# Two-layer hybrid decoder trunk: the memory keys and values of each layer move from the start of the program into the z products of their layer

## The chip, the cores and the metric

The kernel runs on one core of one Trainium2 chip. The metric is the device time of one execution in microseconds, the median of several runs, lower is better. A core has TensorE (PE in the profile, with its weight loads as PEld), VectorE (DVE), ScalarE (ACT), GpSimd (POOL) and SyncE (SP), which here does nothing but issue DMAs. Each engine works through its own list of instructions in the order in which the program was built, and waits where an operand isn't there yet.

## The reference, cut to what matters

```python
def reference(x, mem, ...):
    for l in range(DEPTH):                                   # 2 layers
        h = rms_norm(x, norm_mix_w[l])                       # x: 1024 tokens x 1024
        x = x + hybrid_mixer(h, w_in[l], ...)                # ONE combined projection, three head groups
        hq = rms_norm(x, norm_xq_w[l])
        mem_n = rms_norm(mem, norm_mem_w[l])                 # mem: 256 tokens x 1024, the same in both layers
        x = x + memory_cross_attention(hq, mem_n, w_mq[l], w_mk[l], w_mv[l], w_mo[l])
    return rms_norm(x, final_norm_w)

def memory_cross_attention(h, mem_n, wq, wk, wv, wo):
    k = (mem_n @ wk).reshape(b, m, MEM_HEADS, MEM_HEAD_DIM)  # the memory keys
    v = (mem_n @ wv).reshape(b, m, MEM_HEADS, MEM_HEAD_DIM)  # the memory values
    ...
```

The memory keys and values depend on nothing but `mem` and weights, so they can be computed at any time before the cross-attention of their layer. The mixer's combined projection gives, among others, the values of two attention groups (V), the inputs of the forget gates and time steps, and z, the gate of the state-space group, which is not wanted until that group's output is gated.

## The kernel before, in words

**Products.** Every float32 operand is split into a high and a low half (`hi` on ACT, L77 or, with a scale, L79; `lo` = operand minus `hi`, L85 on POOL or DVE, L83 on DVE with a scale), and a product is three matmuls, high by high, low by high, high by low (`mm3`, L111 to L113; in `tokmaj` L372 to L374). Weights come through `wload`: one 128x1024 tile in two halves of 256 KB, DMA to `wst`, cast to `whi`, the rest to `wlo`. The normed activations of all 1024 tokens are kept as `hhi` and `hlo`, 8 slices k of 128 channels each.

**Order.** `body` runs `start`, then per layer `tokmaj`, `mixer`, `tail`. PE's order is fixed by the program: `weave(main, fill)` runs generators that yield after a few matmuls the time these take; `ratio` says how much of the fill is laid between steps of the main, and with `drain=False` what is left of the fill goes on later. The other engines' lists, SP's included, are laid out by the builder from a simulated timeline. SP issues the DMAs one after another, with up to 8 of them in flight; one that waits holds up all behind it.

**`start` (L1497).** First comes the memory: one tile of `w_mk`, `memT` in four pieces of 256 KB into `mt` (kept for both layers), `memkv(0)` and then `memkv(1)` as the fill under `norms()`. `norms` computes the memory's sums of squares (`memnorm`, L1192), loads x in two halves of eight 256 KB tiles, and norms each half (`norm_half`: squares on ACT, sums on DVE, matmuls with `onecol` L221, then `spread`: a power on POOL L234, diagonals on DVE, a matmul with `ones` L251; then `normed`, whose `lo` alternates between POOL and DVE). `memkv` (L1229) per layer: 8 key tiles of 24 matmuls 128x256, then 4 value pieces for 2 chunks of memory tokens, 24 matmuls each, 384 in all; into the `acc` and `big` buffers of PSUM; the weights alternate between the common pool (`wst`, `whi`, `wlo`) and one of its own (`xst`, `xhi`, `xlo`), and `alt_w` puts the `lo` of every second half on DVE. The results go to DRAM (`mk_hi`, `mk_lo`, `mv_hi`, `mv_lo`).

**`tokmaj` (L346).** Weights of five pieces (`load(pc)`: four DMAs `tms`, casts `tmh` on ACT, rests `tml` on POOL; pieces 0 and 1 are V, 2 to 4 are z). Each piece is multiplied for eight chunks of 128 tokens, 24 matmuls each, alternating between `acc` and `big`. V of tokens 0 to 511 (`values(0)`) is woven with a pending norm, then V of the rest, then `gates` with z as fill, which is drained at the end. A chunk of z is evacuated by a tanh on ACT (L392) and a DVE step (L393) into `zt`, and stored by SP (`z_st`). `gates` ends with sixteen stores of its rows `gar` to `sr_st` and `sl_st`.

Of the kernel before, what the change touches and what calls it, by code (L numbers as in the profile page):

```python
# [16 lines left out]
P = 128  # L17
D = 1024
T = 1024
L = 2  # L20
# [23 lines left out]
class Net:  # L44
# [49 lines left out]
    def wload(self, src, pool=None, first=None):  # L94
        parts = []
        for s in range(2):
            wp, tag, n = (self.wp, "w", 5) if pool is None else (pool, "x", 3)
            st = self.tile(wp, [P, 512], F32, tag + "st", 3)
            self.dma(st, src[:, s * 512 : (s + 1) * 512])
            if first is not None and s == 0:  # L100
                self.dma(first, self.a["memT"][:, 0:2, :])
            hi = self.tile(wp, [P, 512], F32R, tag + "hi", n)
            lo = self.tile(wp, [P, 512], F32R, tag + "lo", n)
            self.hi(hi, st)
            self.lo(lo, st, hi, eng=self.nc.vector if self.alt_w and s or first is not None else self.nc.gpsimd)
            parts.append((hi, lo))
        return parts
# [237 lines left out]
    def tokmaj(self, l, pools, first, norm):  # L345
# [3 lines left out]
        with self.pool("tm", 2, side="right") as pool:  # L349
# [56 lines left out]

            load(0)
            load(1)
            self.run(first)
            self.ratio, self.nb, self.alt_w = 0.0, 1, False  # L410
            self.weave(norm, values(0))
            pools.close()
# [3 lines left out]
            self.weave(self.gates(l), gate_z())  # L416
# [775 lines left out]
    def memnorm(self, pool, tmp):  # L1192
        nc = self.nc
        mt = self.mt
        nch = MT // P
        sums = []
        for k in range(0, KT, 2):
            sq = [self.tile(tmp, [P, MT], F32, "msq", 8) for _ in range(2)]
            nc.scalar.activation(sq[0], mt[:, k, :], AF.Square)
            nc.gpsimd.tensor_tensor(out=sq[1], in0=mt[:, k + 1, :], in1=mt[:, k + 1, :], op=ALU.mult)  # L1200
            nc.vector.tensor_tensor(out=sq[0], in0=sq[0], in1=sq[1], op=ALU.add)
            sums.append(sq[0])
# [6 lines left out]
        self.mrr = yield from self.spread(tmp, ps, nch, self.tile(pool, [P, MT], F32, "mrr", 1))  # L1209
# [3 lines left out]
    def memw(self, l, pool):  # L1213
        w = self.mw[l]
        if l == 0:

            nhi, nlo = (h[:, :, HALF : HALF + MT] for h in (self.hhi, self.hlo))
        else:
            nhi, nlo = (self.tile(pool, [P, KT, MT], F32R, n, 1) for n in ("nhi", "nlo"))
        for k in range(KT):  # L1220
            self.hi(nhi[:, k, :], self.mt[:, k, :], w[:, k : k + 1])
            self.lo(nlo[:, k, :], self.mt[:, k, :], nhi[:, k, :], w[:, k : k + 1])
        return nhi, nlo


    def memkv(self, l, pool, w0):
        nc, a = self.nc, self.a
        mm = nc.tensor.matmul
        nhi, nlo = self.memw(l, pool) if l == 0 else self.mnext  # L1229
        todo = []  # L1230

        def acc(i):
            return self.acc() if i % 2 else self.big()

        def keys(t, ps):
# [8 lines left out]

        def values(pc, c, ps):
            r = self.mrs[:, c : c + 1]
            vh = self.tile(pool, [P, MT], F32R, "kh")
            vl = self.tile(pool, [P, MT], F32R, "kl")
            self.hi(vh, ps, r)
            self.lo(vl, ps, vh, r)  # L1250
            self.dma(self.mvDs[l][0][:, c, pc * MT : (pc + 1) * MT], vh)
            self.dma(self.mvDs[l][1][:, c, pc * MT : (pc + 1) * MT], vl)

        def put(fn, *args):
            todo.append((fn, args))
            while todo and self.mrr is not None:
                g, b = todo.pop(0)
                g(*b)

        for t in range(KT):  # L1260
            ws = w0[t] if t < len(w0) else self.wload(a["w_mk"][l, t], (None, pool)[t % 2])
            ps = acc(t)[:, :MT]
            for k in range(KT):
                whi, wlo = ws[k // 4]
                s = slice((k % 4) * P, (k % 4 + 1) * P)
                self.mm3(ps, whi[:, s], wlo[:, s], nhi[:, k, :], nlo[:, k, :], k == 0, k == KT - 1)
                yield 0.33
            put(keys, t, ps)
        if l + 1 < L:
            self.dma(self.mw[l + 1], a["norm_mem_w"][l + 1])  # L1270
            self.mnext = self.memw(l + 1, pool)
        for pc in range(4):
            ws = self.wload(a["w_mv"][l, pc, 0]) + self.wload(a["w_mv"][l, pc, 1], pool)
            for c in range(2):
                ps = acc(c)[:, :MT]
                cs = slice(c * P, (c + 1) * P)
                for k in range(KT):
                    whi, wlo = ws[k // 2]
                    s = slice((k % 2) * MT, (k % 2 + 1) * MT)
                    mm(ps, nhi[:, k, cs], whi[:, s], start=k == 0, stop=False)  # L1280
                    mm(ps, nhi[:, k, cs], wlo[:, s], start=False, stop=False)
                    mm(ps, nlo[:, k, cs], whi[:, s], start=False, stop=k == KT - 1)
                    yield 0.33
                put(values, pc, c, ps)
# [338 lines left out]
```

## Time and profile before

| | |
|---|---|
| time, median of 3 runs | 2539.09 us (2537.62 to 2541.44) |
| the profiled execution's own time | 2551.32 us |
| its span in the profile | 2549.3 us |
| mean granted clock of TensorE | 0.984 |
| busy PE / DVE / ACT / POOL | 97% / 61% / 47% / 46% |
| first V product of layer 0 | 143.8 us |
| end of the gates, layer 0 and layer 1 | 228.9 and 1424.6 us |

Times are counted from the start of the span. A row of a timeline gives the start in us, the duration in us, the engine, the line of the program, the operation, result<-operands, the tile and how many of them came in a row; in square brackets stands how long the engine had idled before and what ended that. A row of grouped instructions gives their count, then the busy time in us and the mean of one in ns, then the idle time before them and what ended it. A row of windows gives the stretch, its length, the busy time of PE, PEld, DVE, ACT and POOL (with their instructions), the granted clock of TensorE (1.00 is full), the mean busy share of the 16 DMA engines and what they moved in GB/s.

### The profile page before, as it was taken

Reading aid. Unit: us, or ns where it says so; the run is one execution under the profiler, and the core shown is the slowest. Engines: PE = TensorE matmul, PEld = TensorE weight load, DVE = VectorE, ACT = ScalarE, POOL = GpSimd, SP = SyncE. Lnnn points to the kernel's source line nnn. Section 1 sums busy time; section 2 is a strip of 40 time slices with the busy share of each in tenths; the row PEclk is TensorE's granted clock in tenths of the full one; section 3 lists DMA queues with packets and bytes.
Section 4 is the critical chain, followed back from the end, with each engine's and each line's share of the span. In section 5 each row is a group of like instructions: output and inputs, shape, how many; then the busy total and the mean of one; then the engine's idle time right before and its main releaser. Section 6 shows DMA issues by size and latency. Waiting matters only on the chain.

```text
span 2549.3 us, 39348 instructions
## 1 busy us (share of the span) xinstructions
PE 2466.7 (97%) x13900; PEld 2081.7 (82%) x13900; DVE 1545.4 (61%) x2716; ACT 1189.0 (47%) x2455; POOL 1166.9 (46%) x1193
## 2 busy tenths in 40 slices
PE   8799999999999999999999999999999999999997
PEld 7799988888788777888879988888877877787886
DVE  6923166666778688654464226666668868764355
ACT  5532155545556455434443225455546645543442
POOL 5732144435566487432252124444446657732233
PEclk9999999999999999999999999999999999999999
DMA  7774132222222766553464223222223376554333
GB/s 235 217 237 111 65 98 70 66 88 86 81 87 90 246 221 195 162 169 116 128 195 120 78 68 92 70 79 84 89 71 90 115 256 209 170 185 151 119 93 132
DMA packets 230360, 333.37 MB, mean 131 GB/s; under 512 B 24370, under 2 KB 107442, under 8 KB 230148
## 3 DMA queue, kind: packets, MB, share of 16 engines
q1 hardware_dynamic: 228292, 328.76, 41.4%
q8 instruction: 110, 1.80, 0.3%
q10 hardware_dynamic: 1872, 2.10, 0.2%
q14 instruction: 86, 0.70, 0.1%
HBM read 238.72 MB, written 86.81 MB: 128 GB/s over the span
## 4 chain that ended last, share of the span: by engine, by line
PE 78%; DVE 7%; DMA 5%; issue 3%; ACT 3%; POOL 3%; SPq 1%; DVEq 0%; POOLq 0%; ACTq 0%
PE acc L111 16%; PE acc L112 15%; PE acc L113 15%; PE tp L667 3%; PE tp L630 2%; PE acc L372 2%; PE big L372 2%; PE acc L374 2%; PE big L374 2%; PE acc L373 2%; PE big L373 2%; SPq L72 1%; PE big L598 1%; PE big L599 1%; PE s L1128 1%
## 5 line engine op out<-in xcount | busy, mean ns | idle before, releaser
L111 PE MATMUL acc<-hhi,whi 128*128 128x512 f32 (+1 forms) x1960 | 796.8, 407 | 6.8 <-DVE th L510 5.4
L113 PE MATMUL acc<-hlo,whi 128*128 128x512 f32 (+1 forms) x1960 | 772.0, 394 | 0.0
L112 PE MATMUL acc<-hhi,wlo 128*128 128x512 f32 (+1 forms) x1960 | 771.6, 394 | 0.0
L85 POOL TENSOR_TENSOR wlo<-wst,whi 128x512 fp32r<-128x512 f32 x279 | 377.5, 1353 | 337.5 <-ACT whi L77 280.7
L113 PEld LDWEIGHTS acc<-hlo,whi 128*128 128x128 f32 x1960 | 372.0, 190 | 82.2
L111 PEld LDWEIGHTS acc<-hhi,whi 128*128 128x128 f32 x1960 | 374.2, 191 | 67.3 <-DVE th L510 5.8
L112 PEld LDWEIGHTS acc<-hhi,wlo 128*128 128x128 f32 x1960 | 373.8, 191 | 57.7
L77 ACT CAST whi<-wst 128x512 fp32r<-128x512 f32 x420 | 259.5, 618 | 302.8 <-PE acc L113 206.0
L77 ACT CAST ph<-tp 128x512 fp32r<-128x512 f32 (+1 forms) x256 | 142.5, 556 | 168.8 <-PE tp L630 118.0
L85 DVE TENSOR_TENSOR pl<-tp,ph 128x512 fp32r<-128x512 f32 (+1 forms) x256 | 167.0, 652 | 78.3 <-ACT ph L77 76.3
L85 DVE TENSOR_TENSOR wlo<-wst,whi 128x512 fp32r<-128x512 f32 x141 | 128.4, 910 | 118.0 <-ACT whi L77 117.2
L609 POOL TENSOR_SCALAR Pt<-Pt,sm 128x128 f32<-128x128 f32 (+7 forms) x128 | 105.8, 827 | 182.6 <-DVE sm L608 180.0
L1015 DVE SCALAR_TENSOR_TENSOR ac<-u,cw,ac 128x512 f32<-128x512 f32 x144 | 129.4, 899 | 34.0 <-POOL ac L1010 32.6
L85 POOL TENSOR_TENSOR tml<-tms,tmh 128x684 fp32r<-128x684 f32 (+3 forms) x40 | 67.4, 1703 | 132.7 <-ACT tmh L77 126.8
L607 ACT ACTIVATE Pt<-big,sm 128x128 f32<-128x128 f32 (+7 forms) x128 | 95.2, 743 | 69.8 <-DVE sm L605 62.3
L604 DVE TENSOR_REDUCE sm<-big 128x1 f32<-128x128 f32 (+7 forms) x128 | 96.1, 751 | 23.0 <-PE big L601 21.7
L372 PE MATMUL acc<-tmh,hhi 128*128 128x342 f32 (+3 forms) x320 | 102.1, 319 | 0.0
L372 PE MATMUL big<-tmh,hhi 128*128 128x342 f32 (+3 forms) x320 | 101.9, 318 | 0.0
L374 PE MATMUL acc<-tmh,hlo 128*128 128x342 f32 (+3 forms) x320 | 101.4, 317 | 0.0
L373 PE MATMUL big<-tml,hhi 128*128 128x342 f32 (+3 forms) x320 | 101.4, 317 | 0.0
L374 PE MATMUL big<-tmh,hlo 128*128 128x342 f32 (+3 forms) x320 | 101.4, 317 | 0.0
L373 PE MATMUL acc<-tml,hhi 128*128 128x342 f32 (+3 forms) x320 | 101.4, 317 | 0.0
(339 smaller groups left out, 5151.1 us busy)
## 6 DMA issues: line engine op xcount, KB each, us to landing
wst<-in_w_fm_dram SPq DMA_DIRECT2D x132, 256.0 KB
wst<-in_w_out_dram SPq DMA_DIRECT2D x128, 256.0 KB
wst<-in_w_mq_dram SPq DMA_DIRECT2D x64, 256.0 KB
wst<-in_w_mo_dram SPq DMA_DIRECT2D x64, 256.0 KB
xt<-x_st SPq DMA_DIRECT2D x48, 256.0 KB
v_st<-vt SPq DMA_DIRECT2D x32, 320.0 KB
vs<-v_st SPq DMA_DIRECT2D x20, 512.0 KB
xs_st<-tr SPq DMA_DIRECT2D x40, 256.0 KB
```

Of the source, the lines that this page charges most:

```text
L77: self.nc.scalar.copy(out, in_)
L85: (eng or self.nc.vector).tensor_tensor(out=out, in0=in_, in1=f(hi), op=ALU.subtract)
L111: mm(ps, ahi, bhi, start=first, stop=False)
L112: mm(ps, alo, bhi, start=False, stop=False)
L113: mm(ps, ahi, blo, start=False, stop=last)
L372: mm(ps[:, :n], self.hhi[:, k, cs], hi[:, k, :n], start=k == 0, stop=False)
L373: mm(ps[:, :n], self.hhi[:, k, cs], lo[:, k, :n], start=False, stop=False)
L374: mm(ps[:, :n], self.hlo[:, k, cs], hi[:, k, :n], start=False, stop=k == KT - 1)
L604: nc.vector.tensor_reduce(out=sm[:, 0:1], in_=S[:, :n], axis=AX.X, op=ALU.max)
L607: nc.scalar.activation(Pt[:, :n], S[:, :n], AF.Exp, bias=sm[:, 1:2], scale=1.0, accum_out=sm[:, 2:3])
L609: nc.gpsimd.tensor_scalar(out=Pt[:, :n], in0=Pt[:, :n], scalar1=sm[:, 3:4], scalar2=1.0, op0=ALU.mult, op1=ALU.mult)
L1015: nc.vector.scalar_tensor_tensor(ac, u[:, 5 + j : 5 + j + HALF], w[:, t, j : j + 1], ac, ALU.mult, ALU.add)
```

## The change

`start` no longer has anything of the memory in it. It loads the eight tiles of the first half of x at once (14 buffers instead of 8), makes the constants, and gives `tokmaj` two generators: `first` loads the second half and norms the first, `second` norms the second half, woven with `values(0)`. `tokmaj` calls `load(0)` ahead of `first` and `load(1)` behind it, sets `alt_w` to False from the beginning, doesn't drain z after the gates, and then weaves `memkv(l)` of its own layer, as the main part with ratio 1.2, with what is left of z. `memkv` loads the memory's norm weights `mw` and `memT` again in each layer, through three buffers `mt` in four pieces, computes the sums of squares in layer 0 (with `memnorm` ahead of its keys), accumulates in the two `tp` buffers of PSUM and takes all weights from the common pool; both memory token chunks of a value piece now share one pass over the weights. The products themselves, their number and their sizes are the same.

```diff
     def tokmaj(self, l, pools, first, norm):
...
+            self.alt_w = False
             load(0)
+            self.run(first)
             load(1)
-            self.run(first)
-            self.ratio, self.nb, self.alt_w = 0.0, 1, False
+            self.ratio = 0.0
             self.weave(norm, values(0))
+            self.nb = 1
...
             self.run(values(1))
-            self.weave(self.gates(l), gate_z())
+            fill = gate_z()
+            self.weave(self.gates(l), fill, drain=False)
+            self.ratio = 1.2
+            with self.pool("kv", 2) as kv:
+                self.weave(self.memkv(l, kv), fill)
...
+    def memkv(self, l, pool):
         nc, a = self.nc, self.a
         mm = nc.tensor.matmul
...
+        w = self.load_w(pool, a["norm_mem_w"][l], KT, "mw")
+        nhi, nlo = (self.tile(pool, [P, KT, MT], F32R, n, 1) for n in ("nhi", "nlo"))
+        sums = []
+        for k in range(0, KT, 2):
+            mt = self.tile(pool, [P, 2, MT], F32, "mt", 3)
+            self.dma(mt, a["memT"][:, k : k + 2, :])
+            if l == 0:
+                sq = [self.tile(pool, [P, MT], F32, f"msq{i}", 4 - 2 * i) for i in range(2)]
+                nc.scalar.activation(sq[0], mt[:, 0, :], AF.Square)
+                nc.gpsimd.tensor_tensor(out=sq[1], in0=mt[:, 1, :], in1=mt[:, 1, :], op=ALU.mult)
+                nc.vector.tensor_tensor(out=sq[0], in0=sq[0], in1=sq[1], op=ALU.add)
+                sums.append(sq[0])
+            for i in range(2):
+                j = k + i
+                self.hi(nhi[:, j, :], mt[:, i, :], w[:, j : j + 1])
+                self.lo(nlo[:, j, :], mt[:, i, :], nhi[:, j, :], w[:, j : j + 1])
+        yield (self.clock + 8.0,)
+        if l == 0:
+            yield from self.memnorm(pool, sums)
+
+        for t in range(KT):
+            ws = self.wload(a["w_mk"][l, t])
+            ps = self.tp()[:, :MT]
+            for k in range(KT):
+                whi, wlo = ws[k // 4]
+                s = slice((k % 4) * P, (k % 4 + 1) * P)
+                self.mm3(ps, whi[:, s], wlo[:, s], nhi[:, k, :], nlo[:, k, :], k == 0, k == KT - 1)
+                yield 0.35
...
         for pc in range(4):
...
+            pss = [self.tp()[:, :MT] for _ in range(2)]
+            for q in range(2):
+                ws = self.wload(a["w_mv"][l, pc, q])
...
     def start(self):
...
+        def load(half):
+            c = slice(half * HALF, (half + 1) * HALF)
+            accs = self.tile(pool, [P, HALF], F32, "nac", 2)
+            xs = []
+            for m in range(KT):
+                xt = self.tile(pool, [P, HALF], F32, "xt", 14)
+                self.dma(xt, a["xT"][m, :, c])
+                xs.append(xt)
+                self.sqadd((pool, "nsq", 3), accs, xt, m == 0, HALF)
+            sums.append((xs, accs))
+
+        load(0)
         self.constants()
...
         self.dma(self.ident, a["ident"])
...
+        def first():
+            load(1)
+            yield from self.norm_half(pool, *sums[0], wn, 0)
+
+        def second():
+            self.setup()
+            yield from self.norm_half(pool, *sums[1], wn, 1)
+
+        return pools, first(), second()
```

The new kernel also reserves 1024 bytes for descriptors that POOL would write (`dynamic_dma_scratch_size=1024`).

How the lists of the engines change, at three places:

POOL at the start of the program. Before it has the squares of the memory (`msq`), rests of the memory weights (`xlo`, `wlo`) and the power of the memory's norm (`nrs_222`):

```order
L1200 TENSOR_TENSOR msq_191<-mt_101 128x256
L1200 TENSOR_TENSOR msq_196<-mt_101 128x256
L1200 TENSOR_TENSOR msq_201<-mt_101 128x256
L1200 TENSOR_TENSOR msq_206<-mt_101 128x256
L85 TENSOR_TENSOR xlo_174<-xst_171,xhi_173 128x512
L85 TENSOR_TENSOR wlo_251<-wst_248,whi_250 128x512
L85 TENSOR_TENSOR xlo_288<-xst_285,xhi_287 128x512
L85 TENSOR_TENSOR wlo_374<-wst_371,whi_373 128x512
L234 TENSOR_TENSOR nrs_222<-nms_220,mhalf_124 128x2
```

Now it has rests of V's weights (`tml_153` is piece 0, `tml_262` piece 1), the power of the first half's norm (`nrs_217`), rests of the first `w_mk` tiles (`wlo`), and then the rests of the normed x (`hlo`, of which a V product reads all eight slices):

```order
L85 TENSOR_TENSOR tml_153<-tms_154,tmh_152 128x688
L85 TENSOR_TENSOR tml_153<-tms_158,tmh_152 128x688
L231 TENSOR_TENSOR nrs_217<-nms_215,mhalf_145 128x4
L85 TENSOR_TENSOR tml_153<-tms_162,tmh_152 128x688
L85 TENSOR_TENSOR wlo_1382<-wst_1379,whi_1381 128x512
L85 TENSOR_TENSOR wlo_1388<-wst_1385,whi_1387 128x512
L85 TENSOR_TENSOR wlo_1427<-wst_1424,whi_1426 128x512
L85 TENSOR_TENSOR tml_153<-tms_166,tmh_152 128x688
L85 TENSOR_TENSOR tml_262<-tms_263,tmh_261 128x2x320
L85 TENSOR_TENSOR hlo_72<-ntm_229,hhi_71 128x512
L85 TENSOR_TENSOR tml_262<-tms_267,tmh_261 128x2x320
L85 TENSOR_TENSOR hlo_72<-ntm_237,hhi_71 128x512
```

The memory's squares have gone from here, and V's weights and the first half of x stand in POOL's list from its first row. Two more `wlo`, two more `tml_262` and the last two `hlo` follow.

SP behind the gates of layer 1. Before, the last of the sixteen stores of the gates' rows (`gar`), then stores of z and the next weights of z (`tms`):

```order
L72 DMA sl_st_10_80<-gar_2823_14590 4x1024
L72 DMA sr_st_11_81<-gar_2823_14590 4x8x128
L72 DMA z_st_5_75<-zt_2824_14614 128x342
L72 DMA z_st_5_75<-zt_2826_14643 128x342
L72 DMA tms_2856_14940<-in_w_tm4_dram 128x2x340
L72 DMA z_st_5_75<-zt_2828_14672 128x342
L72 DMA z_st_5_75<-zt_2836_14719 128x342
L72 DMA z_st_5_75<-zt_2838_14748 128x342
```

Now, behind the same stores, the memory's norm weights (`mw`) and the first three pieces of the memory (`mt`) stand behind two z stores, and the fourth behind one more z store and a tile of z's weights:

```order
L72 DMA sl_st_10_80<-gar_2673_13871 4x1024
L72 DMA sr_st_11_81<-gar_2673_13871 4x8x128
L72 DMA z_st_5_75<-zt_2681_13926 128x342
L72 DMA z_st_5_75<-zt_2683_13955 128x342
L72 DMA mw_2674_13895<-in_norm_mem_w_dram 128x8
L72 DMA mt_2677_13899<-in_memT_dram 128x512
L72 DMA mt_2678_13905<-in_memT_dram 128x512
L72 DMA mt_2679_13911<-in_memT_dram 128x512
L72 DMA z_st_5_75<-zt_2685_13984 128x342
L72 DMA tms_2819_14721<-in_w_tm4_dram 128x2x340
L72 DMA mt_2680_13917<-in_memT_dram 128x512
```

The loads of the memory are new here, and in the list they come behind the gates' stores and z's.

PE at the same stretch of layer 1, some 50 matmuls behind the last of the gates. Before, one chunk of z (`acc_14647`) ends and the next (`big_14694`) begins:

```order
L373 MATMUL acc_14647<-tml_14360,hhi_71 128x342
L374 MATMUL acc_14647<-tmh_14359,hlo_72 128x342
L372 MATMUL big_14694<-tmh_14676,hhi_71 128x342
L373 MATMUL big_14694<-tml_14677,hhi_71 128x342
L374 MATMUL big_14694<-tmh_14676,hlo_72 128x342
```

Now, six matmuls into that chunk (here `big_14006`), the first key tile comes (`tp_14025`), which reads the split memory `nhi` and `nlo`:

```order
L369 MATMUL big_14006<-tmh_13988,hhi_71 128x342
L370 MATMUL big_14006<-tml_13989,hhi_71 128x342
L371 MATMUL big_14006<-tmh_13988,hlo_72 128x342
L108 MATMUL tp_14025<-nhi_13897,whi_14015 128x256
L109 MATMUL tp_14025<-nhi_13897,wlo_14016 128x256
L110 MATMUL tp_14025<-nlo_13898,whi_14015 128x256
```

That is 57 matmuls of z behind the gates' last. Two and a half key tiles then follow without z between them; after that steps of key and value products and of z alternate by threes, and the last 48 matmuls of z stand behind the last memory product. In layer 0 the same happens 81 matmuls of z after the gates, with the eight 128x1 matmuls on the memory's sums of squares first, 18 more matmuls of z in an unfinished and 18 in a new chunk behind them, then the matmuls that spread the norm, then 4.6 key tiles alone.

135 lines of the change are left out of this document (30 added, 105 removed).

## The prediction

> **What bounds the kernel now.** I read the page first, for who is busy and what the chain that ended last is made of:
>
> ```profile
> span 2549.3 us, 39348 instructions
> PE 2466.7 (97%) x13900; PEld 2081.7 (82%) x13900; DVE 1545.4 (61%) x2716; ACT 1189.0 (47%) x2455; POOL 1166.9 (46%) x1193
> PE 78%; DVE 7%; DMA 5%; issue 3%; ACT 3%; POOL 3%; SPq 1%; DVEq 0%; POOLq 0%; ACTq 0%
> ```
>
> TensorE is the bound: the chain is 78% PE. Whatever the change does, the number of products stays; what can move is the time in which PE stands still or runs at a lower clock. So I look at the stretches it touches: the start, up to the first V product, and for comparison a stretch of z products.
>
> ```profile
> 0.00:143.80 143.80, 115.54 (x806) 111.24 (x807) 107.44 (x143) 82.11 (x161) 89.36 (x73) 0.93 0.74 231
> 250.00:260.00 10.00, 10.00 (x66) 10.00 (x65) 1.02 (x2) 1.05 (x3) 0.00 (x0) 1.00 0.14 53
> L372 PE MATMUL big<-tmh,hhi x8: 318/320/323, 143.8 to 147.1; 128*128 128x344 f32 x8
> 30.05 0.28 PE L111 MATMUL acc<-hhi,xhi 128*128 128x256 f32 x1
> 32.92 0.28 PE L111 MATMUL big<-hhi,whi 128*128 128x256 f32 x1
> ```
>
> The first V product stands at 143.8 us. The two key tiles begin 2.87 us apart, for 24 matmuls 128x256: 0.1196 us each, so the 768 matmuls of both layers are worth 91.8 us. The other 52 us ahead of V are norms, waits and low clock, with DMA at 0.74 and 231 GB/s. In z the matmuls come 66 in 10 us, 0.152 us each, with DMA at 0.14 and POOL idle: room to take work in.
>
> **The start.** The change takes away the 143.8 us; in its place PE waits for x, its norm and V's weights. Rows for that:
>
> ```profile
> 0.00:10.00 10.00, 3.10 (x10) 2.49 (x11) 4.38 (x10) 5.98 (x13) 2.80 (x8) 1.00 0.76 254
> L77 ACT CAST tmh<-tms 128x688 fp32r<-128x688 f32 x4 | 3.1, 770 | 2.6 <-DMA tms<-in_w_tm_dram 2.5
> L85 POOL TENSOR_TENSOR tml<-tms,tmh 128x688 fp32r<-128x688 f32 x4 | 6.7, 1680 | 0.2 <-ACT tmh L77 0.2
> L85 POOL TENSOR_TENSOR tml<-tms,tmh 128x640 fp32r<-128x640 f32 x4 | 6.3, 1569 | 1.4 <-ACT tmh L77 1.0 <-ACT fdt L387 0.4
> L85 POOL TENSOR_TENSOR wlo<-wst,whi 128x512 fp32r<-128x512 f32 x20 | 29.4, 1468 | 16.0 <-ACT whi L77 16.0
> L85 POOL TENSOR_TENSOR hlo<-ntm,hhi 128x512 fp32r<-128x512 f32 x8 | 13.5, 1687 | 8.0 <-ACT hhi L77 6.7 <-DMA mv_hi<-kh 1.3
> L234 POOL TENSOR_TENSOR nrs<-nms,mhalf 128x4 f32<-128x4 f32 x2 | 2.5, 1234 | 1.6 <-DVE nms L232 1.6
> ```
>
> Half of x (2.1 MB), `ident` and the first 0.35 MB piece of V's weights come first, 2.5 MB: at the 254 GB/s of the first row 10 to 10.8 us; the cast takes 0.77, so POOL begins at about 11.6. The order of the changed kernel puts on POOL, ahead of the last `hlo` that the first V chunk reads: 4 `tml` of 128x688 (6.7), the power (1.2), 5 `wlo` (7.3), 4 `tml` of 128x640 (6.3) and 4 `hlo` (6.7; the other four are on DVE), 28.3 us, so 39.9. I add 1.5 for idle while the first `w_mk` tile, far behind in the queue (5.2 MB, about 20 us), is awaited: 41.4. Four matmuls at half clock then end the first chunk at 42.6; less its own warm 24 x 0.152 = 3.6, that is 39.0 of loss ahead of V, and 2.7 for the slow clock after the first matmuls (next fence): 41.7. Bounds: 37, if POOL never waits and V's weights come sooner; 47, if DMA delivers the rest as slowly as the 231 GB/s of the whole start and POOL waits for each `wlo`. I take 41.7, by the durations of these very operations.
>
> What a pause costs in clock, beside its own length:
>
> ```profile
> 43.73 0.58 PE L112 MATMUL acc<-hhi,xlo 128*128 128x256 f32 x1 [2.69 <-DVE xlo L85]
> 43.70:49.70 6.00, 5.97 (x28) 5.97 (x29) 2.62 (x5) 2.37 (x5) 0.00 (x0) 0.50 0.75 231
> 126.95 0.58 PE L1281 MATMUL big<-xlo,nhi 128*128 128x256 f32 x1 [4.54 <-DVE xlo L85]
> 126.90:131.60 4.70, 4.64 (x21) 4.65 (x22) 4.04 (x6) 2.37 (x5) 1.67 (x1) 0.50 0.78 218
> ```
>
> After pauses of 2.69 and 4.54 us the clock stood at 0.50 for 6.0 and 4.7 us, which loses half of that, 3.0 and 2.35: 2.7 a pause. The Trainium skill (TensorE: Matmul & The Clock Gate, Part 1: The HAM clock gate) has the clock halved after an idle window of about 3.4 us and back after one busy window of that length, and warns of idle gaps longer than that; it speaks against this change, which makes such gaps. By it a pause would cost 1.7 us of clock, and the three pauses here together some 2.5 us less than I reckon; the rows agree in kind, but the clock also fell after a pause of 2.69 us and stayed down longer, and I keep to the rows.
>
> **The memory's products** keep their 91.8 us; they now lie in `tp` and alternate with z. Norm matmuls that were under the memory's fill now stand alone:
>
> ```profile
> 101.74 1.02 PE L221 MATMUL tp<-onecol,nac 128*128 128x1 f32 x8 [2.36 <-DVE nac L265]
> 108.63 1.10 PE L251 MATMUL tp<-ndg,ones 128*128 128x512 f32 x2 [0.17 <-DVE ndg L242]
> 16.70 3.41 PE L1206 MATMUL tp<-onecol,msq 128*128 128x1 f32 x16
> L251 PE MATMUL tp<-ndg,ones 128*128 128x256 f32 x2 | 0.4, 278 | 0.0
> ```
>
> The second half's norm is in V (1.0 + 1.1); the memory's is in z (16 small ones, 1.7 at full clock, and 0.4): 4.2.
>
> **The wait in layer 0.** PE's order puts the memory's sums of squares 81 matmuls of z behind the gates, whether or not the memory has been loaded. The stretch before:
>
> ```profile
> 228.91 0.42 PE L372 MATMUL acc<-tmh,hhi 128*128 128x342 f32 x1
> 238.19 1.18 SPq L72 DMA_DIRECT2D z_st<-zt  x2
> 239.78 0.38 SPq L72 DMA_DIRECT2D tms<-in_w_tm_dram  x1
> 242.23 3.89 SPq L72 DMA_DIRECT2D z_st<-zt  x3
> 243.34 0.76 ACT L77 CAST tmh<-tms 128x680 fp32r<-128x680 f32 x1 [1.08 <-DMA tms<-in_w_tm_dram]
> L1200 POOL TENSOR_TENSOR msq<-mt 128x256 f32<-128x256 f32 x4 | 3.2, 823 | 7.0 <-DMA mt<-in_memT_dram 7.0
> L1201 DVE TENSOR_TENSOR msq<-msq,msq 128x256 f32<-128x256 f32 x4 | 3.2, 789 | 0.0
> ```
>
> PE would be there at 228.9 + 81 x 0.152 = 241.2. SP is past its two z stores at 239.4; only then come `mw` and three of the memory's four pieces, each issue about 0.4. The tile of `tms` was used 3.2 us after its issue (240.16 to 243.34), so the first piece lands at about 243.2. The fourth waits for its buffer, which the first frees after squares, `nhi` and `nlo`, about 244.8; it lands at 248.0, and a square (0.8) and part of the last sum bring 249.0. That is 7.8 us of waiting and 2.7 of clock: 10.5. Queued behind PE's wait are the rest of z and the key tiles, so nothing hides it.
>
> **The wait in layer 1.** No sums here, but the first key tile reads all eight slices of `nhi` and `nlo`, 57 matmuls behind the gates:
>
> ```profile
> 1424.55 0.42 PE L372 MATMUL acc<-tmh,hhi 128*128 128x342 f32 x1
> 1426.43 3.80 SPq L72 DMA_DIRECT2D sr_st<-gar  x5
> 1430.34 2.46 SPq L72 DMA_DIRECT2D sl_st<-gar  x7
> 1433.90 1.17 SPq L72 DMA_DIRECT2D z_st<-zt  x2
> 1435.42 0.41 SPq L72 DMA_DIRECT2D tms<-in_w_tm_dram  x1
> 1439.26 0.76 ACT L77 CAST tmh<-tms 128x680 fp32r<-128x680 f32 x1 [1.28 <-DMA tms<-in_w_tm_dram]
> L79 ACT ACTIVATE nhi<-mt,mw 128x256 fp32r<-128x256 f32 x8 | 3.3, 501 | 0.0
> L83 DVE SCALAR_TENSOR_TENSOR nlo<-mt,mw,nhi 128x256 fp32r<-128x256 f32 x8 | 7.3, 981 | 0.0
> ```
>
> PE arrives at 1424.55 + 57 x 0.152 = 1433.2, and would end that tile at 1436.1. SP works off the gates' stores until 1433.9 (sixteen of them; the groups of five and seven alone take 6.3 us) and is past the z stores at 1435.1; the first piece is issued by about 1435.9 and lands at 1439.2 (the `tms` tile took 3.4). Two `nhi` (0.5 each) and the `nlo` behind them free its buffer, the fourth is issued by 1440.8, lands at 1444.0, and the last split and matmuls end at 1445.6: a wait of 9.5. The products of the early pieces come between, so part of the slow clock lies under the waiting; I count half of the 2.7: 10.9.
>
> **Costed at nothing.**
>
> ```profile
> L85 POOL TENSOR_TENSOR kl<-kf,kh 128x256 fp32r<-128x256 f32 x16 | 14.9, 935 | 8.9 <-DMA mk_lo<-kl 8.3 <-ACT whi L77 0.5
> ```
>
> All `lo` of the memory's weights on POOL: 32 x 1.47 a layer and 8 `kl` of 0.94, 54.5 us, beside 46 us of memory products and about as much z; without that cover it would show in key tiles alone (a rival). Loading `memT` twice is 1 MB in stretches where DMA is at 0.14. The first norm's `nb` of 3 in place of 1, the unwritten scratch, `mw` on SP rather than ACT (one issue, counted above) change no term. The mixer's first weights are behind the memory's, but 48 matmuls of z, 7.3 us, stand between. The second half's norm is due at about 71 us, when V reaches its tokens, and its x has landed by 25.
>
> Sum: 41.7 + 91.8 + 4.2 + 10.5 + 10.9 = 159.1, against 143.8: +15.3, so the span goes from 2549.3 to 2564.6. The profiled execution took 2551.32 us, 12.2 above the median of 2539.09; those 12 us are spread and I can't place them, so I carry the difference to the median: 2554.4.
>
> **The rivals.** *The memory is there in time (0.13).* If SP gets to the pieces 8 to 10 us sooner, both waits and their clock go (21.4): 159.1 - 21.4 = 137.7, -6.1, 2533.0, faster. For it: the stores are tiny, and the order is laid out by a timeline in which they may be short. Against: SP's rows above, the same in both layers. *Half the waits (0.15).* The profiled execution is the slower one; if the stores drain 5 us earlier without the profiler, each wait falls by 5 and the clock's share by half (2.0 in all): 147.1, +3.3, 2542.4, the same within 0.2%. *POOL is late in key tiles alone (0.12).* A key tile takes POOL 2 x 1.47 + 0.9 = 3.9 us and PE 2.9. Layer 0 has 4.6 such tiles in a row, layer 1 2.5, with 2.5 staged ahead; if none of the staging holds, two tiles of 1.0 are late in each layer: +4.2, 2558.6, and it decides only if the `wst` tiles come late too. *The price of the start* is no rival but a bound, 37 to 47.
>
> **How the numbers follow.** Forecast, with its own reading of the waits, 0.60: 2554.4. A measurement of this kernel tells a change from none at about 0.2%, 5.1 us. Faster: only the first rival, 0.13. The same: the second, 0.15. Slower: the forecast and the third, 0.72. The low end has a start of 37 and half of each wait: 37 + 91.8 + 4.2 + 5.2 + 5.4 = 143.6, 2538.9, so 2539. The high end has a start of 47 and the fourth piece one z store later (the three stores took 3.9 us), 13 each: 47 + 91.8 + 4.2 + 26 = 169.0, +25.2, 2564.3; I say 2565. The first rival is left out, and some of the tails.
>
> **What would show it.** Right: the first V chunk ends at about 42.6 us, with POOL busy ahead of it; in layer 0 a wait of 6 to 10 us at the 128x1 matmuls on `msq`, released by a chain from `mt`; in layer 1 waits at `tp<-nhi` and `tp<-nlo` that add up to 8 to 11, with 0.50 clock behind both; SP past the gates' stores at the same distance from the gates as before. Wrong: a first V chunk that ends past 48 or before 38; memory pieces landed before PE arrives; pauses inside the key tiles for `wlo`; a z part that is longer than its products plus these waits.

## The result, and the profile after

The changed kernel takes 2560.97 us (median of 6 runs, 2558.02 to 2569.26) against 2541.24 (6 runs, 2537.62 to 2543.49): a ratio of 1.0086, 95% interval 1.0071 to 1.0101, slower. The page of its profile begins so:

```profile
span 2556.8 us, 39371 instructions
PE 2451.3 (96%) x13900; PEld 2068.0 (81%) x13900; DVE 1515.2 (59%) x2683; ACT 1191.0 (47%) x2455; POOL 1203.9 (47%) x1226
```

The busy sums tell little. The stages do: windows of the changed kernel, cut at the end of the first V chunk, at the first z product behind the gates and three matmuls (0.7 us) into the mixer's products, for both layers (columns: stretch, length, busy time of PE, PEld, DVE, ACT and POOL with their instructions, clock, DMA share, GB/s).

```profile
0.00:49.67 49.67, 13.68 (x42) 10.79 (x43) 37.28 (x37) 24.93 (x40) 32.10 (x23) 1.00 0.63 207
49.67:136.56 86.89, 84.10 (x542) 82.05 (x541) 40.32 (x72) 22.20 (x53) 20.71 (x13) 1.00 0.49 142
136.56:266.27 129.71, 120.09 (x841) 119.07 (x841) 28.30 (x57) 42.88 (x86) 56.53 (x52) 0.95 0.47 136
266.27:1384.85 1118.58, 1101.29 (x6098) 912.05 (x6096) 710.92 (x1264) 547.33 (x1134) 537.49 (x554) 0.99 0.41 130
1384.85:1509.40 124.55, 117.52 (x823) 116.21 (x823) 23.65 (x46) 41.44 (x80) 53.61 (x47) 0.97 0.46 142
1509.40:2556.80 1047.40, 1014.66 (x5560) 827.80 (x5558) 674.69 (x1210) 512.23 (x1063) 503.42 (x538) 0.99 0.40 125
```

The gates of layer 0 end at 136.56 instead of 228.91. Then the z stretch takes 129.71 and in layer 1 124.55; before it was 69.05 in both (next section). The memory's products are worth 45.9 us a layer, so each stretch should be 114.95, with some 2 us more in layer 0 for the memory's norm; the clock of 0.95 and 0.97 and a PE that is busy for 120.09 of 129.71 show where the rest is. (The 1.00 of the first row isn't borne out by its matmuls: those of 128x344 take 0.49 us up to 53.1 and 0.32 from there on.)

**The start.** Four TensorE rows, then DVE and POOL of the changed kernel, up to the end of the first V chunk; last, the rests `hlo` that DVE made in the whole run from `ntm` and from `tp` (shortest, middle and longest in ns, then when):

```profile
36.01 0.65 PE L371 MATMUL big<-tmh,hlo 128*128 128x344 f32 x1 [1.55 <-POOL hlo L85]
44.93 0.66 PE L371 MATMUL big<-tmh,hlo 128*128 128x344 f32 x1 [5.10 <-POOL hlo L85]
49.38 0.49 PE L371 MATMUL big<-tmh,hlo 128*128 128x344 f32 x1
49.67 0.49 PE L369 MATMUL acc<-tmh,hhi 128*128 128x344 f32 x1
...
43.67 1.75 DVE L85 TENSOR_TENSOR hlo<-ntm,hhi 128x512 fp32r<-128x512 f32 x1
47.79 0.69 DVE L85 TENSOR_TENSOR hlo<-ntm,hhi 128x512 fp32r<-128x512 f32 x1 [0.68 <-ACT hhi L77]
...
26.48 4.16 POOL L85 TENSOR_TENSOR tml<-tms,tmh 128x688 fp32r<-128x688 f32 x2 [2.76 <-ACT tmh L77]
35.91 3.39 POOL L85 TENSOR_TENSOR wlo<-wst,whi 128x512 fp32r<-128x512 f32 x2
39.27 3.92 POOL L85 TENSOR_TENSOR tml<-tms,tmh 128x640 fp32r<-128x640 f32 x2
43.16 3.40 POOL L85 TENSOR_TENSOR hlo<-ntm,hhi 128x512 fp32r<-128x512 f32 x2
...
L85 DVE TENSOR_TENSOR hlo<-ntm,hhi x32: 679/693/2025, 29.2 to 2345.7; 128x512 fp32r<-128x512 f32 x32
L85 DVE TENSOR_TENSOR hlo<-tp,hhi x32: 676/691/693, 1131.0 to 2491.3; 128x512 fp32r<-128x512 f32 x32
```

As forecast, TensorE waits for the last `hlo` on POOL behind rests that V's first chunk doesn't read. What the forecast left out is that the two engines slow each other. On DVE the same operation takes 1.75 us while POOL works and 0.69 when POOL is idle; DVE, which makes the other half of `hlo` and all of `ntm`, is busy for 37.28 of the 49.67 us. On POOL a `wlo` takes 1.7 us here and a `tml` of 128x640 2.0, where the forecast's rows had means of 1.47 and 1.57; all 72 `wlo` of this run with DVE idle beside them took 1.27 to 1.31. The Trainium skill (GPSIMD Engine Reference, 1. Specifications) has POOL's access to SBUF shared with DVE, with contention for DVE instructions that read two inputs from SBUF; the rows agree. The rests that read `tp`, a buffer of PSUM, never took more than 0.693, though POOL was busy through the whole of 16 of the 32.

**The wait in layer 0.** TensorE, then SP, then DVE and POOL:

```profile
155.46 0.56 PE L1202 MATMUL tp<-onecol,msq 128*128 128x1 f32 x2 [5.89 <-DVE msq L1224]
160.92 2.29 PE L1202 MATMUL tp<-onecol,msq 128*128 128x1 f32 x10 [3.08 <-DVE msq L1224]
...
147.35 1.20 SPq L72 DMA_DIRECT2D z_st<-zt  x2
149.27 1.38 SPq L72 DMA_DIRECT2D mt<-in_memT_dram  x3
155.06 0.33 SPq L72 DMA_DIRECT2D mt<-in_memT_dram  x1
...
159.04 1.83 DVE L1224 TENSOR_TENSOR msq<-msq,msq 128x256 f32<-128x256 f32 x1 [1.05 <-POOL msq L1223]
158.96 1.62 POOL L85 TENSOR_TENSOR tml<-tms,tmh 128x680 fp32r<-128x680 f32 x1
```

TensorE stops at 149.57 and has the last sum at 160.92: 9.0 us in two waits (and 0.5 between them), with the fourth piece issued at 155.06, and the last sum on DVE 1.83 us long beside POOL. **Layer 1:**

```profile
1400.12 0.58 PE L108 MATMUL tp<-nhi,whi 128*128 128x256 f32 x1 [6.05 <-ACT nhi L79]
1406.54 0.39 PE L110 MATMUL tp<-nlo,whi 128*128 128x256 f32 x1 [0.80 <-DVE nlo L83]
...
1396.15 1.37 SPq L72 DMA_DIRECT2D mt<-in_memT_dram  x3
1401.01 0.33 SPq L72 DMA_DIRECT2D mt<-in_memT_dram  x1
```

The key tiles behind these waits run without a pause in both layers: POOL's rests are never late there.

### The profile page after: what moved, and what is told of

The parts are those of the page before. It is cut to its first block, busy times and chain, and to the rows that moved or that the text cites. A ratio compares the mean times of both kernels' runs of the same rounds, so it can differ in the third digit from the quotient of the medians.

```text
span 2556.8 us, 39371 instructions
## 1 busy us (share of the span) xinstructions
PE 2451.3 (96%) x13900; PEld 2068.0 (81%) x13900; DVE 1515.2 (59%) x2683; ACT 1191.0 (47%) x2455; POOL 1203.9 (47%) x1226
## 4 chain that ended last, share of the span: by engine, by line
PE 76%; DVE 8%; DMA 6%; issue 3%; POOL 3%; SPq 2%; ACT 2%; DVEq 0%; POOLq 0%; ACTq 0%
PE acc L108 15%; PE acc L109 15%; PE acc L110 15%; PE tp L670 3%; SPq L72 2%; PE tp L633 2%; PE acc L369 1%; PE acc L371 1%; PE acc L370 1%; PE big L371 1%; PE big L369 1%; PE big L370 1%; PE s L1131 1%; PE big L601 1%; PE big L602 1%
## 5 line engine op out<-in xcount | busy, mean ns | idle before, releaser
L85 POOL TENSOR_TENSOR wlo<-wst,whi 128x512 fp32r<-128x512 f32 x328 | 437.5, 1335 | 415.2 <-ACT whi L77 347.1
L77 ACT CAST whi<-wst 128x512 fp32r<-128x512 f32 x452 | 279.5, 618 | 365.6 <-PE acc L110 196.3
L85 DVE TENSOR_TENSOR wlo<-wst,whi 128x512 fp32r<-128x512 f32 x124 | 113.6, 916 | 104.5 <-ACT whi L77 103.8
L371 PE MATMUL big<-tmh,hlo 128*128 128x342 f32 (+3 forms) x320 | 103.2, 323 | 10.5 <-POOL hlo L85 10.5
```

The lines of the kernel that those rows point to most:

```text
L77: self.nc.scalar.copy(out, in_)
L85: (eng or self.nc.vector).tensor_tensor(out=out, in0=in_, in1=f(hi), op=ALU.subtract)
L371: mm(ps[:, :n], self.hlo[:, k, cs], hi[:, k, :n], start=False, stop=k == KT - 1)
```

## The experiments

Theory at the outset: the 20 us are the two waits, the memory being late because its loads stand behind the gates' stores in SP's queue. Rivals: the products run badly between z; the start costs more than reckoned; the profiles differ by chance.

### The kernel before, a second profile

> The kernel before, once more, for a second profile. In the two profiles at hand the stages that the change doesn't touch (from the first mixer product of a layer to the end of its tail) are 8.0 and 8.3 us longer before than after, beside 27.2 against 13.7 us and then less of granted clock 0.50 in them. If that is only the draw of one execution, this profile has those stages within 3 us of the changed kernel's (1119.3 us from the first mixer product of layer 0 to the first z product behind the gates of layer 1, against 1127.3 in the first profile), a span near 2541 and fewer half-clock stretches. If the change itself made the stages shorter (rival), they are 8 us longer here again.

Measured: 2536.45 us. Its windows, cut as above:

```profile
0.00:142.40 142.40, 115.57 (x806) 111.48 (x807) 107.31 (x143) 82.06 (x161) 89.92 (x73) 0.93 0.74 234
142.40:227.49 85.09, 85.09 (x565) 83.80 (x563) 26.86 (x59) 21.34 (x49) 23.16 (x15) 1.00 0.62 183
227.49:296.54 69.05, 69.05 (x439) 68.92 (x439) 11.98 (x22) 12.39 (x24) 6.93 (x7) 1.00 0.19 57
296.54:1417.22 1120.68, 1099.09 (x6098) 909.78 (x6096) 713.38 (x1264) 547.72 (x1134) 537.13 (x554) 1.00 0.41 130
1417.22:1486.27 69.05, 69.05 (x440) 68.92 (x439) 11.90 (x22) 12.33 (x24) 6.93 (x7) 1.00 0.19 57
1486.27:2534.60 1048.33, 1017.83 (x5560) 830.50 (x5558) 673.46 (x1210) 512.60 (x1063) 504.12 (x538) 0.99 0.39 125
```

The stages that the change doesn't touch are 1120.68 and 1048.33 here, 2.1 and 0.9 longer than in the changed kernel; the first profile had them 8.0 and 8.3 longer. So the change didn't make them shorter: the first profile had drawn a long execution. Against this second profile the account closes: gates 90.9 earlier, z stretches 60.7 and 55.5 longer, the rest 3.0 shorter, together +22.2, which is 2556.8 less 2534.6.

### The loads ahead of the gates

```diff
-            with self.pool("kv", 2) as kv:
-                self.weave(self.memkv(l, kv), fill)
+            with self.pool("mm", 1) as mp:
+                self.mw = self.load_w(mp, self.a["norm_mem_w"][l], KT, "mw")
+                self.mts = [self.tile(mp, [P, 2, MT], F32, "mt", 4) for _ in range(4)]
+                for k in range(4):
+                    self.dma(self.mts[k], self.a["memT"][:, 2 * k : 2 * k + 2, :])
...
```

> The changed kernel with the memory's four pieces and its norm weights loaded ahead of the gates in each layer, into four buffers of their own; TensorE's order is the same. Theory: what the change costs is the wait for the memory, which is late because its loads stand behind the gates' sixteen stores in SP's queue; from the gates' end to the first mixer product the changed kernel has 60.7 us more than before in layer 0 and 55.5 in layer 1, of which the products are 45.9 each. Without the wait that is at most 50 and 48 us more, the time falls by 15 to 21 us, to about 2542, level with the kernel before. Rival: the products themselves run badly between z (POOL's low halves, two buffers of PSUM): then both stretches stay within 3 us and so does the time.

Measured: 2559.66 us, ratio to before 1.0089 (1.0074 to 1.0105): nothing gained. The stretches fell by only 2.9 and 2.3 us, to 126.77 and 122.21, and the V part before them grew by 3. The theory in this form has fallen, and these are the numbers that the rival gave; the next run tells whether it is right. What TensorE waits for now, in layer 0 and in layer 1 (first row PE, layer 0; then ACT and DVE, layer 1):

```profile
156.57 1.23 PE L1207 MATMUL tp<-onecol,msq 128*128 128x1 f32 x4 [4.29 <-ACT tmh L77]
...
1395.89 2.08 ACT L77 CAST tmh<-tms 128x680 fp32r<-128x680 f32 x3 [3.36 <-DMA sl_st<-gar]
1397.87 3.30 ACT L79 ACTIVATE nhi<-mt,mw 128x256 fp32r<-128x256 f32 x8
...
1398.41 8.38 DVE L83 SCALAR_TENSOR_TENSOR nlo<-mt,mw,nhi 128x256 fp32r<-128x256 f32 x8 [5.34 <-ACT nhi L79]
```

The memory has long landed, but its splits stand in ACT's list behind three casts of z's last weights, whose buffer TensorE has to free first, and DVE then takes 8.38 us for eight `nlo`, 1.05 each, beside POOL. That is a second chain, almost as late as the loads. (The profile names a store for the casts' wait; in the kernel before, the same casts waited for TensorE. In layer 0 it names a later cast for TensorE's wait, which ended 0.1 us behind the `msq` that the matmul reads.)

### The products later

```diff
-        yield (self.clock + 8.0,)
+        yield (self.clock + 24.0,)
         if l == 0:
             yield from self.memnorm(pool, sums)
```

> The changed kernel with one number changed: memkv first lets 24 us of z pass on TensorE, not 8, so the first memory product stands about 120 matmuls of z later. The loads stay where they are in SP's queue. Theory (late loads): the wait is covered by z that would have come later, the time falls by 13 to 20 us, and the pauses ahead of the memory's sums and of the first key tile are under 1 us. Rival (products run badly between z): no z is left to lay between the last value pieces, so the time falls by less than 5 us or rises.

Measured: 2538.03 us, ratio 0.9998 (0.9984 to 1.0011): 22.9 us under the changed kernel, all of the loss and more than the theory gave. Windows of the two z stretches, cut as above:

```profile
136.37:253.34 116.97, 116.77 (x841) 116.10 (x841) 28.40 (x55) 42.10 (x85) 55.02 (x49) 1.00 0.47 142
1377.02:1491.67 114.65, 114.65 (x823) 114.04 (x823) 23.27 (x46) 40.51 (x80) 53.50 (x47) 1.00 0.52 154
```

116.97 and 114.65, against 114.95 for products without any wait (and about 2 for the norm in layer 0), at full clock, though the last 39 memory matmuls of layer 0 have no z between them. The rival (products run badly between z) is out. The stretches are 12.7 and 9.9 us shorter than in the changed kernel, together 22.6 of the 22.9. The memory is as late as ever; TensorE does z meanwhile.

### The memory prepared ahead of the gates

```diff
+            with self.pool("mm", 1) as mp:
+                mem = self.memkv(l, mp)
+                next(mem)
+                self.weave(self.gates(l), fill, drain=False)
...
-            mt = self.tile(pool, [P, 2, MT], F32, "mt", 3)
+            mt = self.tile(pool, [P, 2, MT], F32, "mt", 2)
```

The squares are all made on ACT and added up in one tile here, so the memory's norm takes 2 small matmuls instead of 8.

> The changed kernel with the memory not only loaded but squared, summed and split (nhi, nlo) ahead of the gates; its products stand about where the change puts them, 36 matmuls of z behind the gates in layer 0, even sooner than in the changed kernel. The run with early loads alone lost only 2.9 and 2.3 us of the two stretches, since the splits still stood on ACT behind three casts of z's last weights, which wait for TensorE to free their buffer, and took 5.6 to 8.4 us on DVE beside POOL. Theory: what costs is that the split memory is late by whatever queue, SP's first, ACT's and DVE's next; with all of it ahead of the gates the stretches from the gates' end to the mixer fall from 129.7 and 124.6 us to 115 to 118 each and the time by 18 to 23 us. Rival: key tiles so early in z run badly by themselves; then the stretches stay above 122.

Measured: 2551.34 us, ratio 1.0044 (1.0030 to 1.0059). One window of this run (layer 1), and what was left in layer 0 (PE, then POOL):

```profile
1385.42:1499.55 114.13, 114.13 (x822) 113.67 (x820) 18.53 (x38) 36.98 (x72) 53.49 (x47) 1.00 0.49 146
...
156.08 0.83 PE L248 MATMUL tp<-ndg,ones 128*128 128x256 f32 x2 [5.80 <-DVE ndg L239]
...
149.77 4.78 POOL L85 TENSOR_TENSOR tml<-tms,tmh 128x680 fp32r<-128x680 f32 x3 [18.74 <-DMA sl_st<-gar]
154.50 0.70 POOL L231 TENSOR_TENSOR nrs<-nms,mhalf 128x2 f32<-128x2 f32 x1
```

In layer 1 the wait is gone with the products early: it was the split memory, not the place. In layer 0 the stretch is 122.81, above what the theory gave and on the rival's side of 122; but the one pause in it over 0.3 us is the one shown: the power of the memory's norm stood on POOL behind three rests of z's last weights, a 5.80 us wait on a third list. Half of the loss is recovered, not all as the theory had it, and the gates came 3.5 us later.

### The start without foreign rests

```diff
+            if l == 0:
+                for _ in range(3):
+                    nc.vector.tensor_copy(self.tile(pool, [P, 2, W], F32, "tms", 3)[:, 0, :1], f(self.hlo[:, KT - 1, HALF - 1 : HALF]))
             load(1)
...
+            for _ in range(3):
+                self.nc.vector.tensor_copy(self.tile(self.wp, [P, 512], F32, "wst", 3)[:, :1], f(self.hlo[:, KT - 1, HALF - 1 : HALF]))
```

> The changed kernel with POOL's rests of the first w_mk tiles and of V's second piece held back until the first half of x is split (six tiny copies into the three wst and three tms buffers, which read the last slice of hlo); nothing else is changed. Theory for the start: the first V chunk ends at 49.7 us rather than the forecast 42.6 because these nine operations (about 14 us) share the time of POOL and DVE with the split of x; without them it ends at 38 to 41 us and the time falls by 8 to 11 us, with the waits in z as they were. Rival: the start is bound by the transfers and by DVE's own chain (sums, ntm), then it ends at 46 or later and the time moves by less than 4 us.

Measured: 2554.56 us, ratio 1.0074 (1.0057 to 1.0092). TensorE's rows for the last matmul of the first V chunk and for a new wait:

```profile
40.38 0.49 PE L371 MATMUL big<-tmh,hlo 128*128 128x344 f32 x1
59.58 0.42 PE L370 MATMUL big<-tml,hhi 128*128 128x320 f32 x1 [3.03 <-POOL tml L85]
```

The chunk ends at 40.7, 9.0 sooner, as expected: POOL's foreign rests and what they do to DVE were the cause (the run doesn't part the two). But the gates come only 3.8 sooner: 3.0 went to a wait for V's second weights. The time is 6.4 us under the changed kernel's by the medians, not the 8 to 11 of the theory, and the two ratios' intervals overlap.

### Later products with a lighter start

The first variant holds back the `w_mk` tiles alone, until the second half of x is split; the second holds back V's second piece as well, as in the edit above.

```diff
+            self.hold = [self.tile(self.wp, [P, 512], F32, "wst", 3) for _ in range(3)]
...
             yield from self.norm_half(pool, *sums[1], wn, 1)
+            for t in self.hold:
+                self.nc.vector.tensor_copy(t[:, :1], f(self.hlo[:, KT - 1, T - 1 : T]))
```

> The run with the memory products 24 us behind the gates, and on top of it the three wst buffers held until the second half of x is split, so POOL has no rests of w_mk tiles at the start. V's second piece is prepared early, as in the changed kernel. In the run with both held back the first V chunk ended 9.0 us sooner (40.7 against 49.7), but 3.0 us went to a wait for the rests of V's second piece and the gates came only 3.8 us sooner. Theory: without the five w_mk rests (8.3 us of POOL, and DVE beside it) the first V chunk ends at 43 to 45 and nothing is given back: the gates 4 to 6 us sooner than in the run with later products, time 2532 to 2535. Rival: the second half's norm is the next bound and gives back all but 2 us.

Measured: 2537.39 us, ratio 0.9992 (0.9978 to 1.0005); the chunk ends at 45.3, the gates come 1.9 sooner than in the run with later products (134.52 against 136.37). The rival's size, though by other waits, for ACT (2.72, the one shown below) and for DVE (2.21).

> As the run before it, and V's second piece held back until the first half of x is split as well; with no w_mk rests between, POOL makes its four rests at once behind the power of the second half's norm. Theory: first V chunk ends at about 40.7, the rests of the second piece are there by 48 to 50, before TensorE needs them at about 55, so nothing is waited for: the gates 7 to 9 us sooner than in the run with later products, time 2529 to 2532. Rival: DVE and POOL are then late with the second half's norm (POOL's four rests push its split back), TensorE waits for it at token 512, and the gates come no more than 4 us sooner.

Measured: 2535.57 us, ratio 0.9980 (0.9969 to 0.9991): faster than the kernel before, though by less than the theory had it. The chunk ends at 39.7, the gates come at 133.04, only 3.3 sooner. The rival named the wrong wait. TensorE, ACT and SP:

```profile
99.88 0.64 PE L369 MATMUL acc<-tmh,hhi 128*128 128x320 f32 x1 [6.34 <-ACT fdt L384]
...
97.23 0.21 ACT L478 ACTIVATE gan<-gan 128x16 f32<-128x16 f32 x1 [11.42 <-DMA gan<-in_a_log_dram]
...
79.57 6.95 SPq L72 DMA_DIRECT2D sr_st<-indr  x4
94.20 0.43 SPq L72 DMA_DIRECT2D gan<-in_a_log_dram  x1
```

V's evacuation on ACT stands behind `gan`, a small load for the gates, and that stands in SP's list behind stores of constant rows.

### The constant rows elsewhere

```diff
-                self.dma(self.srD[:, b, 2:10, :].rearrange("c r t -> r c t"), indr[:, None, :].to_broadcast([8, NB, 512]))
...
+            if l == 0:
+                self.fixed_more()
```

`fixed_more` makes those stores: first behind the memory products, then (last run) behind the eighth key tile. The control moves them in the kernel before.

> The run with later products and both held back at the start (first V chunk 9.8 us sooner, gates only 3.3), and on top of it the constant rows that the mixer wants (indr and the ones: eight stores that kept SP for 7 us and more) move behind the memory products; the zeros stay. Theory: the gain of the start was given back at 99.88 us, where TensorE waited 6.3 us for ACT, and ACT for gan, a small load for the gates that stood behind those stores in SP's queue. Without them the wait is under 1 us, the gates come 5 to 7 us sooner (126 to 128), the time falls by 4 to 7 us, to 2529 to 2532. Rival: gan is held up by the stores of V and the zeros as much; then the wait stays over 4 us and the time the same.

Measured: 2534.07 us, ratio 0.9987 (0.9974 to 1.0000). In the profile the wait at the gates is gone and they come at 120.15, 12.9 sooner, twice what the theory gave; but the mixer then waits behind the same stores, `acc<-hhi,whi` at 257.45:

```profile
257.45 0.80 PE L108 MATMUL acc<-hhi,whi 128*128 128x512 f32 x1 [4.64 <-ACT stg L79]
```

The profiled execution was the quickest of its 12 (2524.15); the median doesn't show the gain, and the 2529 to 2532 of the theory wasn't reached. I can't say how much of those 12.9 us other executions have.

> The same move of the constant rows in the kernel before, as a control: its profile shows no pause of TensorE between the first V product and the gates, so nothing is there to gain. Theory: its time stays within 0.15%, and the gates within 1 us of 227.5. Rival: the rows cost time in themselves, wherever they stand; then the kernel before gains as much as the other, 4 us or more.

Measured: 2536.99 us, ratio 1.0003 (0.9990 to 1.0016): the same, as the theory had it. Its second half missed: the gates came 2.5 sooner than in the second profile, not within 1, all of it ahead of the first V product.

> The run with the constant rows late, but with them behind the eighth key tile of layer 0, not behind the last value piece (one copied element of that tile in ones and indr holds them back till then). In the run before it the gates came 12.9 us sooner by the profile (120.1 against 133.0), but the mixer then had a wait of 4.6 us at 257.45, behind the same stores, with the clock at 0.50 for 6.8 us. Theory: between the value pieces SP has room, so there is no wait at the gates, none in the values and none at the mixer's start; the first mixer products of layer 0 at 235 to 238, the time 3 to 8 us under that run's, 2526 to 2531, and faster than the kernel before by 0.2 to 0.4%. Rival: the stores hold up the weights of the value pieces there; then pauses of 3 us or more stand in the values and the time stays.

Measured: 2534.92 us, ratio 0.9987 (0.9974 to 1.0000), not the 2526 to 2531 of the theory. The rival is what happened. TensorE, then ACT, then SP:

```profile
211.72 0.58 PE L1273 MATMUL tp<-whi,nhi 128*128 128x256 f32 x1 [5.70 <-DVE kl L83]
...
210.16 0.62 ACT L77 CAST whi<-wst 128x512 fp32r<-128x512 f32 x1 [8.59 <-DMA wst<-in_w_mv_dram]
...
199.20 2.19 SPq L72 DMA_DIRECT2D sr_st<-indr  x1
204.12 3.86 SPq L72 DMA_DIRECT2D wst<-in_w_mv_dram  x3
```

The weights of the value pieces are late behind the stores. (The profile names DVE for TensorE's wait; the `whi` that the matmul reads was cast at 210.16, after 8.59 us of waiting for its load.) At each of the three places tried, something waits behind these stores. The run with the two pieces held back, which leaves them alone, is the only one whose whole interval is under 1; it is the best of several, and the intervals of the others overlap with it, so no order among them is shown.

## Why the prediction was right, and where it was off

The direction and the two waits were right; the size came out larger, +19.7 us by the medians against +15.3, with 2560.97 inside the range. By its own steps:

- **The start, 41.7: mis-sized.** The first V chunk ended at 49.67, not 42.6, and past the 48 that the prediction itself had named as a sign of being wrong. POOL's list was read rightly, but its last `hlo` was done at 46.56 rather than 41.4: POOL began 0.7 later, stood idle for 3.0 rather than 1.5 us, and worked for 31.3 rather than 28.3, beside a DVE that was itself slowed (1.75 us beside POOL, 0.69 alone). The prices came from rows of the old start, and neither engine's work was costed as slowing the other's. From 26.48 on POOL had no pause, so there it was its own longer operations that counted. The last 1.9 us came behind POOL: small sums of the second half's norm, 1.6 us, stand inside the chunk. Holding the foreign rests back brought the chunk to 40.7. By the gates the start had brought 92.35 us against the first profile, where the forecast's terms (143.8 less 41.7 and 2.1 of the second half's norm) made it 100.0: 7.6 too much, which puts the start at 49.3, above its upper bound of 47. It is the largest of the errors; those of the two z stretches, 60.7 and 55.5 us longer against 58.5 and 56.8 forecast, come to 0.9 together.
- **The products, 45.9 a layer:** 116.97 and 114.65 for the stretches without waits, against 69.05 + 45.9 = 114.95 and the norm in layer 0. Right, and so was costing POOL's rests in them at nothing: the third rival (late POOL in key tiles) didn't happen. The norm in z showed as 2.0, against 2.1.
- **The wait in layer 0, 10.5:** 129.71 less 116.97 is 12.7. The fourth piece was issued 18.5 us behind the gates rather than 15.9, SP being past the gates' stores 1.5 us later than before, and the last sum took 1.83 us on DVE beside POOL.
- **The wait in layer 1, 10.9:** 124.55 less 114.65 is 9.9. Two errors partly cancel in it: the pauses at `nhi` and `nlo` came to 6.9 us, below the 8 to 11 that were to show the forecast right, and the clock behind them (0.66 from 1400.12 to 1407.10) cost more than the 1.4 us reckoned for it.
- **Why the memory is late: half right.** SP's list was as described, but the first rival was wrong to make everything hang on it. With the loads early, ACT and DVE were late by nearly as much; with the splits early, POOL was, in layer 0. Any one of these lists is enough to make TensorE wait, and of the runs here only the later place of the products on TensorE (24 us instead of 8) took all of the wait.
- **From profile to median: sound.** The sum is made of stages that the change touches. The 12.2 us between the profiled execution and the median lay almost all in the others, which the second profile had 13.3 us shorter, so they weren't in the +15.3, and carrying it to the median was right. The forecast span, 2564.6, was missed for the same reason: against the first profile the touched stages came to +23.8, the others to -16.3, so the two first profiles differ by only 7.5 us. Against the second profile the difference is 22.2, by the medians 19.7; the 2.5 between these I can't place.

So the range held in part by luck, the start having left its own bounds: on the touched stages the errors come to 8.5 us, and the time by the medians shows about half of that.

Of the clock rule of the Trainium skill (TensorE: Matmul & The Clock Gate, Part 1: The HAM clock gate) the prediction said that it would make the sum 2.5 us smaller; layer 1 came 1.0 below my figure, layer 0 2.2 above, so these waits don't decide between its price and mine.

What the change set out to do also worked in part: with the waits covered it is level with before, since the start's loss without products (143.8 - 91.8 = 52.0 us) only came back as 51.5 (136.56 less the 85.09 that V takes). What stays open is why the profiled execution of the run with the rows late was 10 us quicker than its median.

## What to carry to other kernels

Work that is moved into a gap needs its operands ready at the new place; read that off every in-order list that prepares them, not just the first one that is late, and if several are, move the consumer rather than chase each. Two engines that work beside each other may slow each other: look for the same operation at two durations, and price a list from rows that had the same neighbour. And never difference two single profiles: compare the stages that the change can't touch first, and take their difference out.

## What the runs showed of the hardware

- A 128x512 rest of `ntm` on DVE took 0.69 us in all 18 rows of the changed kernel in which POOL was idle, and 1.68 to 2.02 in the four in which POOL worked throughout; a rest of `tp`, from PSUM, took 0.69 beside POOL too. POOL's own rest of `ntm` took 1.29 us in the two rows with DVE idle and 1.68 to 1.75 in the seven rows with DVE beside it almost throughout. A cast of 128x4 elements on DVE in the changed kernel's start took 1.62 us at 16.97, beside POOL, and 0.17 at 50.13, without it.
- The kernel before ran between 2529 and 2547 us in the comparisons with the experiments, with mean clocks from 0.984 to 0.992 (its first profiled execution, 2551, lay outside), and the stages with equal work differed by 6 and 7 us between two profiles of it. The Trainium skill (TensorE: Matmul & The Clock Gate, Part 1: The HAM clock gate) says that the clock is judged in free-running windows of about 3.4 us; a pause of 2.22 us, of the same length in both profiles of the kernel before, was followed by a clock of 0.50 in the first (it ends at 1899.07) and of 1.00 in the second (it ends at 1889.01), which fits windows that run freely, though the pause is shorter than the page's window. A change of 0.2% needs many runs of this kernel.
